# Long tails and two-block starts at the seams of a chain of layers: four units of weights held at a part's end, three units of two blocks at its beginning

## The chip, the cores and the metric

The kernel runs on 1 core of one Trainium2 chip. The metric is the time of one execution on the device, in microseconds (us). Engines are named as in the profile: PE is TensorE (PEld its weight loads), DVE VectorE, ACT ScalarE, POOL GpSimd, SP the queue that issues most DMAs.

## The reference

One sequence of 256 tokens with 1024 features, all in float32, goes through two networks of two layers each, one behind the other.

```python
def first_block(x, ...):                       # two layers
    for l in range(2):
        x = x + 0.5 * swiglu_ffn(rmsnorm(x, ffn1_norm[l]), ffn1_w_up[l], ffn1_w_down[l])
        x = x + mixer(rmsnorm(x, mix_norm[l]), w_in[l], b_in[l], ...)
        x = x + 0.5 * swiglu_ffn(rmsnorm(x, ffn2_norm[l]), ffn2_w_up[l], ffn2_w_down[l])
        x = rmsnorm(x, final_norm[l])

def second_block(x, c, ...):                   # two layers, h is scaled and shifted by mod
    mod = silu(c) @ mod_w[i] + mod_b[i]
    h = rms_norm(x, norm_mix_pre[i]) * (1.0 + sc_m) + sh_m
    y = mixer_ab(h, ...) if i == 0 else mixer_c(h, ...)
    x = x + (1.0 + g_m) * rms_norm(y, norm_mix_post[i])
    h = rms_norm(x, norm_ffn_pre[i]) * (1.0 + sc_f) + sh_f
    x = x + (1.0 + g_f) * rms_norm(conv_ffn(h, ...), norm_ffn_post[i])
```

`swiglu_ffn` is `(silu(h @ up_a) * (h @ up_b)) @ down` with 2816 hidden features. `mixer` adds three groups of banded attention and a convolution module: a gated input, a convolution over 31 tokens on 1024 channels, a layer norm over the channels, SiLU and a projection. `mixer_ab` joins a gated linear recurrence (a causal convolution over 4 tokens, two gates by 64x64 blocks, a scan) with a compressed, selected and windowed attention; `mixer_c` is a gated causal convolution over 3 tokens; `conv_ffn` a gated network whose gate passes a causal convolution over 3 tokens.

## The kernel before

Ten **parts** stand in a row: ffn1, mixer, ffn2 for each of two layers, then mixer_ab, conv_ffn, mixer_c, conv_ffn. Each begins with a norm of x, which is held in the tile `xres` as two **halves** of 128 tokens (h0, h1), and ends with a projection whose result is added to x.

Every product with a float32 weight is three matmuls: weights and activations are split into a rounded part (`hi`, `xh`, on ACT or DVE) and a rest (`lo`, `xl`, on DVE or POOL), and hi*xh, lo*xh and hi*xl are summed. A **unit** is four row blocks of 128 by 512 columns of a weight (1 MB): one DMA into `raw` (3 buffers), a cast to `hi`, a subtraction to `lo` (3 buffers of each). The first three units of each part are "fine" (`self.fine`): their `lo` is made by POOL in four quarters of 128x512. One unit is 24 matmuls of 128x512 in the form `xs`, 12 for each half of the tokens, into one sum for each half (tokens by columns). A block of 512 output columns is two units for a weight with 1024 rows, six for ffn's w_down and conv_ffn's down. The form `ws` has the weights stationary and gives columns by tokens, in matmuls of 128x256; where columns by tokens are wanted of an `xs` block, `first_block` copies its result on ACT (L928) and turns it on PE (eight transposes, L931).

A part's seam works thus. `xs_units` runs the last TAIL = 2 units of a projection's second half of columns first for h0 and then for h1, so that h0's norm can start while PE works on h1 (18 matmuls in ffn and conv_ffn, where the last unit has two row blocks, 24 elsewhere). The norm goes over ACT and DVE (sums of squares, `hr`, `rstd`, `xn`), PE transposes `xn` (L264, result `tp`), ACT and DVE make `xh` and `xl` (L269, L270, L276, L278, L279), and the next part's first block starts with two units for h0 and then h1 (`xs_units` with tail 2, or `first_block`). In ffn with `nxt` and `out` (ffn2 of layer 1, before mixer_ab) `scale_x` (L323) scales each half of x for the residual directly behind its `next_xT`.

The order of each engine's instructions is fixed when the kernel is built, by a scheduler that goes by priorities and by the order of the code. Side work is handed out by `pump`, a few tasks behind each unit of weights: the steps of mixer's convolution (L623, DVE, one tap on a channel block each), the `mod` products (L853, DVE, on 1 MB loads of mod_w, in ffn1 and ffn2) and the recurrence's gates in mixer_ab (L1122 on PE, then ACT and DVE). In mixer, ORDER lists the blocks: G a gate of the convolution's input, A its value (with A0 the convolution can begin), two digits or x8 a block of queries, keys or values, a and g, c the attention and the later gates. Behind the convolution stands its layer norm: sums on POOL (L611, `u`), a mean by PE (L716), a subtraction (L719), squares, sums on POOL (`lns`), a sum by PE (L731), and at its end `cTh` (L499), which the convolution's projection needs.

Of the kernel before, what the change touches and what calls it, by code (L numbers as in the profile page):

```python
# [11 lines left out]
F32R = mybir.dt.float32r  # L12
# [16 lines left out]
ORDER = "G0 A0 04 00 G1 A1 02 x8 06 a0 10 g0 16 12 14 a1 g2 g1 c g3".split()  # L29
# [6 lines left out]
TAIL = 2  # L36
# [8 lines left out]
class Net:  # L45
# [78 lines left out]
    def weights(self, src, heads=False):  # L124
# [7 lines left out]
        if not heads:  # L132
            return self.split_raw(raw, kk, n)
# [229 lines left out]
    def xs_units(self, units, tail=0):  # L363
        acc = [self.mmt(), self.mmt()]
        n = len(units)
        tail = min(tail, n)
        for i, (xt, k0, src) in enumerate(units[: n - tail]):
            self.xs(acc, xt, k0, self.weights(src), i == 0, i == n - 1)
        last = [(i, u, self.weights(u[2])) for i, u in enumerate(units) if i >= n - tail]
# [3 lines left out]
        return acc  # L373

# [4 lines left out]
    def ffn(self, norm, w_up, w_down, extra=None, then=None, pre=None, final=None, nxt=None):  # L379
        self.fine = FINE  # L380
        self.cut = 1 if then else None
        out = []
# [3 lines left out]
        with ExitStack() as es:  # L386
            hp = es.enter_context(tc.tile_pool(name="ffnh", bufs=1))
            wp = es.enter_context(tc.tile_pool(name="ffnw", bufs=4))
# [3 lines left out]
            if extra:  # L392
                mp = es.enter_context(tc.tile_pool(name="modp", bufs=1))
# [3 lines left out]
            for c0 in range(0, DFF, 512):  # L397
                n = min(512, DFF - c0)
                ac = {}
                if n < 512:  # L400
# [5 lines left out]
                    ac = {0: acc, DFF: [a[:, n:] for a in acc]}  # L406
                for off in (0, DFF) if n == 512 else ():
                    ac[off] = self.xs_units(self.units(w_up, xt, off + c0, n), TAIL if off + c0 == 0 else 0)
                    if off + c0 == 0:
                        self.cut = None  # L410
                        if then:
                            then()
                        if final is not None:
                            rows = hp.tile([P, D], F32, name="fb")
                            nc.sync.dma_start(rows, final.partition_broadcast(P))
                        self.bg["mod"].extend(tasks)
# [86 lines left out]
    def mixer(self, l, d, xt):  # L503
# [9 lines left out]
        with ExitStack() as es:  # L513
# [24 lines left out]
            def qkv(e, i0, head=False):  # L538
# [5 lines left out]
                acc = [self.mmt(), self.mmt()]  # L544
                ws = []
                for k0 in (0, 4):
                    src = w9[:, k0 : k0 + 4, i0] if both else w9[:, k0 : k0 + 4, i0 : i0 + 2, e]
# [996 lines left out]
```

## Time and profile before

| | us |
|---|---|
| median of 3 runs (2185.32 to 2195.68) | 2190.9 |
| profiled execution | 2186.2 |
| its span | 2184.4 |
| PE busy | 2123.1 (97%) |
| DVE busy | 1433.4 (66%) |
| ACT busy | 1142.0 (52%) |
| POOL busy | 537.4 (25%) |

The table is read from the page of the profiled execution and the times of the runs. PE is busy nearly all the time, so a gain is to be looked for in the stretches in which it isn't, and in those in which its clock is low.

### The profile page before, as it was taken

Reading aid. Unit: us, or ns where it says so; the run is one execution under the profiler, and the core shown is the slowest. Engines: PE = TensorE matmul, PEld = TensorE weight load, DVE = VectorE, ACT = ScalarE, POOL = GpSimd, SP = SyncE. Lnnn points to the kernel's source line nnn. Section 1 sums busy time; section 2 is a strip of 40 time slices with the busy share of each in tenths; the row PEclk is TensorE's granted clock in tenths of the full one; section 3 lists DMA queues with packets and bytes.
Section 4 is the critical chain, followed back from the end, with each engine's and each line's share of the span. In section 5 each row is a group of like instructions: output and inputs, shape, how many; then the busy total and the mean of one; then the engine's idle time right before and its main releaser. Section 6 shows DMA issues by size and latency. Waiting matters only on the chain.

```text
span 2184.4 us, 30473 instructions
## 1 busy us (share of the span) xinstructions
PE 2123.1 (97%) x11966; PEld 1810.9 (83%) x11966; DVE 1433.4 (66%) x2343; ACT 1142.0 (52%) x1578; POOL 537.4 (25%) x431
## 2 busy tenths in 40 slices
PE   8999999999999999999999999999999999999998
PEld 6887988888887788798888888778877998797997
DVE  6844788857877654488876785575555665566663
ACT  5435545565443443554565544576666544546452
POOL 3003985532001200488652200230002000202000
PEclk9999999999999999999999999999999999999999
DMA  9865553437988555466334886565223646554553
GB/s 350 315 205 170 183 191 124 140 135 263 346 302 292 178 177 182 154 197 209 112 111 155 302 315 186 165 158 178 85 78 106 197 144 210 169 188 158 180 177 112
DMA packets 233152, 415.04 MB, mean 190 GB/s; under 512 B 16048, under 2 KB 74288, under 8 KB 233008
## 3 DMA queue, kind: packets, MB, share of 16 engines
q1 hardware_dynamic: 232208, 410.99, 56.2%
q10 hardware_dynamic: 800, 2.10, 0.3%
q8 instruction: 94, 1.54, 0.3%
q14 instruction: 50, 0.41, 0.1%
HBM read 410.94 MB, written 2.11 MB: 189 GB/s over the span
## 4 chain that ended last, share of the span: by engine, by line
PE 88%; DVE 6%; ACT 3%; DMA 2%; issue 1%; POOL 1%; SPq 0%; DVEq 0%; ACTq 0%; POOLq 0%
PE mm L191 18%; PE mm L193 18%; PE mm L192 18%; PE mm L475 8%; PE mm L477 8%; PE mm L476 8%; PE sp L677 2%; PE sp L1330 1%; PE po L692 1%; DMA raw<-in_ffn_w_up 1%; PE tp L428 1%; PE tp L687 1%; DMA mraw<-in_mod_w 1%; PE tp L264 1%; DVE lo L175 1%
## 5 line engine op out<-in xcount | busy, mean ns | idle before, releaser
L171 ACT CAST hi<-raw 128x2048 fp32r<-128x2048 f32 (+2 forms) x427 | 635.8, 1502 | 516.3 <-PE mm L193 295.5
L175 POOL TENSOR_TENSOR lo<-raw,hi 128x512 fp32r<-128x512 f32 x384 | 501.4, 1338 | 1380.5 <-ACT hi L171 1087.8
L175 DVE TENSOR_TENSOR lo<-raw,hi 128x2048 fp32r<-128x2048 f32 (+1 forms) x241 | 531.2, 2205 | 338.1 <-ACT hi L171 335.5
L191 PE MATMUL mm<-hi,xh 128*128 128x512 f32 x1136 | 451.3, 398 | 8.7 <-DVE xh L278 5.3
L193 PE MATMUL mm<-hi,xl 128*128 128x512 f32 x1136 | 450.4, 397 | 1.7 <-DVE xl L270 1.7
L192 PE MATMUL mm<-lo,xh 128*128 128x512 f32 x1136 | 449.1, 395 | 0.6 <-POOL lo L175 0.3
L475 PE MATMUL mm<-xh,hi 128*128 128x256 f32 x1248 | 355.7, 285 | 0.9 <-ACT gc L763 0.4
L477 PE MATMUL mm<-xh,lo 128*128 128x256 f32 x1248 | 354.8, 284 | 0.0
L476 PE MATMUL mm<-xl,hi 128*128 128x256 f32 x1248 | 354.5, 284 | 0.0
L191 PEld LDWEIGHTS mm<-hi,xh 128*128 128x128 f32 x1136 | 216.0, 190 | 56.6 <-DVE xh L278 7.8
L193 PEld LDWEIGHTS mm<-hi,xl 128*128 128x128 f32 x1136 | 215.4, 190 | 48.3 <-DVE xl L270 3.0
L192 PEld LDWEIGHTS mm<-lo,xh 128*128 128x128 f32 x1136 | 216.0, 190 | 46.3 <-POOL lo L175 2.4
L475 PEld LDWEIGHTS mm<-xh,hi 128*128 128x128 f32 x1248 | 239.0, 192 | 2.7 <-ACT gc L763 0.8
L477 PEld LDWEIGHTS mm<-xh,lo 128*128 128x128 f32 x1248 | 239.0, 191 | 2.5 <-issue 1.3
L476 PEld LDWEIGHTS mm<-xl,hi 128*128 128x128 f32 x1248 | 239.1, 192 | 2.4 <-issue 1.3
L623 DVE SCALAR_TENSOR_TENSOR sp<-u,cols,sp 128x256 f32<-128x256 f32 x464 | 225.8, 487 | 7.8
L193 PE MATMUL mm<-hi,hl 128*128 128x512 f32 x528 | 209.9, 397 | 0.0
L191 PE MATMUL mm<-hi,hh 128*128 128x512 f32 x528 | 209.6, 397 | 0.0
L192 PE MATMUL mm<-lo,hh 128*128 128x512 f32 x528 | 209.6, 397 | 0.0
L853 DVE CUSTOM_DVE_ANT_0 mraw<-mraw,cact 128x1024 f32<-128x1024 f32 x96 | 117.6, 1254 | 12.3 <-DMA mraw<-in_mod_w 9.5
L193 PEld LDWEIGHTS mm<-hi,hl 128*128 128x128 f32 x528 | 99.6, 189 | 24.0
L192 PEld LDWEIGHTS mm<-lo,hh 128*128 128x128 f32 x528 | 99.4, 188 | 23.8
(337 smaller groups left out, 2664.8 us busy)
## 6 DMA issues: line engine op xcount, KB each, us to landing
raw<-in_ffn_w_up SPq DMA_DIRECT2D x98, 1024.0 KB, 6.1
raw<-in_ffn_w_down SPq DMA_DIRECT2D x60, 1024.0 KB, 5.0
mraw<-in_mod_w SPq DMA_DIRECT2D x48, 1024.0 KB, 7.2
raw<-in_w_in SPq DMA_DIRECT2D x72, 512.0 KB, 4.5
raw<-in_w_in SPq DMA_DIRECT2D x32, 1024.0 KB, 5.3
raw<-in_ffn_w_gate SPq DMA_DIRECT2D x20, 1024.0 KB, 5.1
raw<-in_ab_w_in SPq DMA_DIRECT2D x18, 1024.0 KB, 5.2
raw<-in_sc_w_in SPq DMA_DIRECT2D x12, 1024.0 KB, 5.1
```

Source lines behind the costliest of these rows:

```text
L171: nc.scalar.copy(hi[:, c : c + hi_step], raw[:, c : c + hi_step])
L175: eng.tensor_tensor(lo[:, bs], raw[:, bs], as32(hi[:, bs]), op=OP.subtract)
L191: nc.tensor.matmul(a, xh[:, k0 + k, t], wh[:, k], start=st, stop=False)
L192: nc.tensor.matmul(a, xh[:, k0 + k, t], wl[:, k], start=False, stop=False)
L193: nc.tensor.matmul(a, xl[:, k0 + k, t], wh[:, k], start=False, stop=en)
L264: nc.tensor.transpose(pt[:, j], src[:, k * P : k * P + P], self.ident)
L475: nc.tensor.matmul(a, wh[:, k, js], xh[:, k0 + k], start=st, stop=False, skip_group_check=True)
L476: nc.tensor.matmul(a, wh[:, k, js], xl[:, k0 + k], start=False, stop=False, skip_group_check=True)
L477: nc.tensor.matmul(a, wl[:, k, js], xh[:, k0 + k], start=False, stop=en, skip_group_check=True)
L623: dv.scalar_tensor_tensor(cv[:, ch] if j == CW - 1 else acc[:, e], src, w, acc[:, e], op0=OP.mult, op1=OP.add)
L677: nc.tensor.matmul(sc[:, o : o + n], QK[e, pr, g, hs], QK[e, pr, 3 + g, ks], start=True, stop=True)
L853: dv.tensor_tensor_reduce(r, r, self.cact, 1.0, 0.0, op0=OP.mult, op1=OP.add, accum_out=self.mod[i][:, 4 * b + 2 * u + j][:, None])
```

## The change

- `xs_units` takes `spare`: two more pairs of buffers for `hi` and `lo`. With them the tail has TAIL + 2 = 4 units. ffn's w_down, conv_ffn's down and mixer_ab's w_out pass it for their second half of columns; mixer's w_out and mixer_c's w_out don't. In ffn the room comes from pools that are closed before w_down (`ffnw` and `modp`, the buffers of `hv` and `mraw`), in mixer_ab from tiles that are done.
- `two_blocks` begins a part: two units of a first block and one of a second for h0, the same three for h1, then the fourth unit for both halves. It begins all four ffn (first blocks of both halves of w_up), mixer (G0 and 04), mixer_ab (both blocks of the recurrence's input), mixer_c and both conv_ffn. `turned_block` turns a finished block. In conv_ffn `up` and in mixer_c `cg` were `ws` blocks and are now `xs` blocks that are turned.
- In mixer G0 and 04 thus come ahead of A0.
- In ffn2 of layer 1 `scale_x` comes behind both halves' `next_xT`.
- In ffn the `mod` tasks are handed over ahead of the load of `final`'s rows.

```diff
-ORDER = "G0 A0 04 00 G1 A1 02 x8 06 a0 10 g0 16 12 14 a1 g2 g1 c g3".split()
+ORDER = "A0 00 G1 A1 02 x8 06 a0 10 g0 16 12 14 a1 g2 g1 c g3".split()
...
-    def xs_units(self, units, tail=0):
+    def xs_units(self, units, tail=0, spare=None):
         acc = [self.mmt(), self.mmt()]
         n = len(units)
-        tail = min(tail, n)
+        spare = deque(spare() if spare else ())
+        tail = min(tail + len(spare), n)
...
+    def two_blocks(self, u0, u1):
+        get = lambda u: u[2]() if callable(u[2]) else self.weights(u[2])
+        accs = [[self.mmt(), self.mmt()] for _ in range(2)]
+        first = [(0, True, u0[0], get(u0[0])), (0, False, u0[1], get(u0[1])), (1, True, u1[0], get(u1[0]))]
+        for h in range(2):
+            for i, start, (xt, k0, _), w in first:
+                self.xs([accs[i][h]], xt, k0, w, start, not start, halves=(h,))
+        self.xs(accs[1], u1[1][0], u1[1][1], get(u1[1]), False, True)
+        return accs
...
+            up.close()
+            tl = es.enter_context(tc.tile_pool(name="ffnt", bufs=1))
             for c in range(2):
                 cs = slice(c * 512, c * 512 + 512)
-                acc = self.xs_units(self.units(w_down, (hh, hl), c * 512, 512), TAIL * c)
+                units = self.units(w_down, (hh, hl), c * 512, 512)
+                acc = self.xs_units(units, TAIL * c, (lambda: self.two_units(tl)) if c else None)
...
                             self.next_xT(nt, h, s, *nxt, xn(), tmp)
-                            if out:
-                                self.scale_x(h, r)
+            if nxt and out:
+                for h in range(2):
+                    self.scale_x(h, out[h][0])
...
+            accs = self.two_blocks(
+                self.units(w_in, xt, 3 * AW + D, 512),
+                [(xt, k0, lambda k0=k0: self.weights4(w9[:, k0 : k0 + 4, 4:6, 0])) for k0 in (0, 4)],
+            )
+            glu_gate(0, self.turned_block(self.tiles(wk, [P, 512], "w", 4), accs[0]))
+            qkv(0, 4, accs[1])
...
+            accs = self.two_blocks(*(self.units(w_in, xs, blk * 512, 512) for blk in range(2)))
             for blk in range(2):
-                a = self.first_block(lambda: work([512], "q"), w_in, xs, blk * 512)
+                a = self.turned_block(lambda: work([512], "q"), accs[blk])
```

How the built order moves, at three places. The first is **SP from ffn2 to ffn1 of the next layer** (layer 0 to 1). `raw` with `in_ffn_w_down` are ffn2's last weights, `mraw` the loads of mod_w for ffn1 of layer 1. Before:

```order
L849 DMA mraw_6107<-in_mod_w 128x2x1024
L131 DMA raw_5520<-in_ffn_w_down 128x4x512
L849 DMA mraw_6141<-in_mod_w 128x2x1024
L131 DMA raw_5550<-in_ffn_w_down 128x4x512
L131 DMA raw_5580<-in_ffn_w_down 128x4x512
L849 DMA mraw_6200<-in_mod_w 128x2x1024
L131 DMA raw_5610<-in_ffn_w_down 128x4x512
```

In the changed kernel:

```order
L131 DMA raw_5779<-in_ffn_w_down 128x4x512
L131 DMA raw_5785<-in_ffn_w_down 128x2x512
L131 DMA raw_6034<-in_ffn_w_up 128x4x512
L131 DMA raw_6046<-in_ffn_w_up 128x4x512
L131 DMA raw_6058<-in_ffn_w_up 128x4x512
L131 DMA raw_6142<-in_ffn_w_up 128x4x512
L853 DMA cact_6202<-in_c 128x1024
L865 DMA mraw_6205<-in_mod_w 128x2x1024
```

All twelve loads of mod_w stood among ffn2's w_down; now they stand behind ffn1's first weights.

The second is **DVE behind the last softmax of mixer** (`sm`, layer 0; layer 1 is the same). `sp` with `u` and `cols`, and `cv` with them, are steps of the convolution, a row with x4 is four of them; `cv` with `sp` is the layer norm's subtraction. Before:

```order
L681 ISA sm_3593,mn_3594<-sp_3589,mask_288 128x512
L681 ISA mn_3594 128x1
L623 SCALAR_TENSOR_TENSOR sp_2429<-u_1546,cols_100,sp_2429 128x256
L500 TENSOR_TENSOR oT_3992<-of_1550,oT_3992 128x512
L623 SCALAR_TENSOR_TENSOR sp_2429<-u_1546,cols_100,sp_2429 128x256
L698 RECIPROCAL rd_3608<-den_3531 128x4
L623 SCALAR_TENSOR_TENSOR cv_1549<-u_1546,cols_100,sp_2429 128x256 x2
L719 TENSOR_TENSOR cv_1549<-cv_1549,sp_3868 128x512
```

In the changed kernel:

```order
L690 ISA sm_3603,mn_3604<-sp_3599,mask_362 128x512
L690 ISA mn_3604 128x1
L636 SCALAR_TENSOR_TENSOR sp_2439<-u_1556,cols_100,sp_2439 128x256
L518 TENSOR_TENSOR oT_4002<-of_1560,oT_4002 128x512
L636 SCALAR_TENSOR_TENSOR sp_2439<-u_1556,cols_100,sp_2439 128x256
L707 RECIPROCAL rd_3618<-den_3541 128x4
L636 SCALAR_TENSOR_TENSOR sp_2439<-u_1556,cols_100,sp_2439 128x256 x5
L709 TENSOR_TENSOR ov_3620<-po_3540,rd_3618 128x256
L636 SCALAR_TENSOR_TENSOR sp_2439<-u_1556,cols_100,sp_2439 128x256 x5
L518 TENSOR_TENSOR oT_4002<-of_1560,oT_4002 128x512
L636 SCALAR_TENSOR_TENSOR sp_2439<-u_1556,cols_100,sp_2439 128x256 x2
L636 SCALAR_TENSOR_TENSOR cv_1559<-u_1556,cols_100,sp_2439 128x256 x2
```

Four steps stood behind the last softmax, now sixteen do. On PE the mean's matmul (L716, now L725) moves back by some sixty rows, while the first matmul with `cTh` keeps its place.

The third is **PE at the beginning of mixer_ab**. `ident,abw` are the transposes of a turned block, `xc,wr` the recurrence's gate of a channel block, which needs that block's finished convolution; rows with `xtW` are the next block, for keys and values. Before, 48 matmuls less seven of block 1 stand between the last transposes of block 0 and these rows:

```order
L193 MATMUL mm_11938<-hi_11953,xl_11322 128x512
L931 MATMUL mm_12005<-ident,abw_12007 128x128 x2
L931 MATMUL mm_12006<-ident,abw_12007 128x128 x2
L1122 MATMUL sp_12107<-xc,wr 64x256
L931 MATMUL mm_12005<-ident,abw_12013 128x128 x2
```

In the changed kernel:

```order
L194 MATMUL mm_11836<-hi_11947,xl_11340 128x512
L958 MATMUL mm_11975<-ident,abw_11977 128x128 x2
L958 MATMUL mm_11976<-ident,abw_11977 128x128 x2
L958 MATMUL mm_11975<-ident,abw_11983 128x128 x2
L958 MATMUL mm_11976<-ident,abw_11983 128x128 x2
L1160 MATMUL sp_12129<-xc,wr 64x256
L958 MATMUL mm_12027<-ident,abw_12029 128x128 x2
L958 MATMUL mm_12028<-ident,abw_12029 128x128 x2
```

Both blocks' matmuls now stand ahead of the turning, so the first gate follows the turning of block 0 with nothing between.

## Rows read from the trace of the kernel before

**Rows 1.** The page: busy us of each engine, share of the span, instructions.

```profile
PE 2123.1 (97%) x11966; PEld 1810.9 (83%) x11966; DVE 1433.4 (66%) x2343; ACT 1142.0 (52%) x1578; POOL 537.4 (25%) x431
```

**Rows 2.** Windows: stretch, its us, busy time by engine, PE clock, DMA share, GB/s.

```profile
201.00:221.00 20.00, 18.06 (x92) 13.73 (x91) 11.69 (x25) 13.77 (x31) 13.80 (x12) 1.00 0.48 158
459.00:475.00 16.00, 12.06 (x81) 11.63 (x80) 10.80 (x13) 12.15 (x15) 0.00 (x0) 0.79 0.58 201
702.00:745.00 43.00, 35.43 (x151) 27.75 (x150) 34.88 (x83) 21.77 (x40) 15.87 (x10) 0.92 0.62 200
...
1402.00:1428.00 26.00, 19.81 (x81) 14.85 (x80) 19.32 (x42) 16.86 (x42) 15.04 (x13) 0.87 0.40 131
1430.00:1462.00 32.00, 32.00 (x166) 22.57 (x164) 29.77 (x63) 25.49 (x48) 13.50 (x15) 1.00 0.77 176
1674.00:1696.00 22.00, 17.61 (x80) 13.15 (x79) 16.64 (x33) 15.71 (x43) 11.72 (x9) 1.00 0.44 139
1876.00:1900.00 24.00, 19.31 (x86) 14.73 (x85) 16.78 (x29) 17.44 (x39) 11.30 (x8) 0.86 0.44 149
1977.00:2002.00 25.00, 20.44 (x89) 15.74 (x88) 17.10 (x29) 17.29 (x40) 11.25 (x8) 0.86 0.39 133
```

**Rows 3.** DVE in order of time, ffn2 to ffn1: start, us, instruction, idle before it.

```profile
700.08 1.89 DVE L853 CUSTOM_DVE_ANT_0 mraw<-mraw,cact 128x1024 f32<-128x1024 f32 x1 [1.69 <-DMA mraw<-in_mod_w]
...
704.12 0.68 DVE L441 SCALAR_TENSOR_TENSOR xres<-mm,xres 128x512 f32<-128x512 f32 x1
705.59 0.69 DVE L336 TENSOR_TENSOR xres<-xres,fb 128x512 f32<-128x512 f32 x1 [0.79 <-ACT junk L207]
```

**Rows 4.** PE in order of time, ffn2 of layer 1 to mixer_ab.

```profile
1402.59 0.39 PE L191 MATMUL mm<-hi,hh 128*128 128x512 f32 x1
...
1406.56 0.40 PE L193 MATMUL mm<-hi,hl 128*128 128x512 f32 x1
1409.26 0.66 PE L264 MATMUL tp<-ident,xn 128*128 128x128 f32 x4 [2.30 <-DVE xn L350]
1410.76 0.63 PE L264 MATMUL tp<-ident,xn 128*128 128x128 f32 x4 [0.84 <-DVE xn L350]
1413.27 0.80 PE L191 MATMUL mm<-hi,xh 128*128 128x512 f32 x1 [1.89 <-DVE xh L278]
```

**Rows 5.** DVE in order of time, the same stretch.

```profile
1402.79 0.69 DVE L441 SCALAR_TENSOR_TENSOR xres<-mm,xres 128x512 f32<-128x512 f32 x1 [7.49 <-PE mm L193]
...
1407.75 2.86 DVE L350 TENSOR_SCALAR xn<-xres,rstf 128x512 f32<-128x512 f32 x2
1410.53 1.88 DVE L323 TENSOR_SCALAR xres<-xres,rstd 128x512 f32<-128x512 f32 x2
...
1421.21 0.88 DVE L350 TENSOR_SCALAR xn<-xres,rstf 128x512 f32<-128x512 f32 x2
```

**Rows 6.** POOL in order of time, the same stretch.

```profile
1406.42 5.32 POOL L175 TENSOR_TENSOR lo<-raw,hi 128x512 fp32r<-128x512 f32 x4 [2.03 <-issue]
1415.22 4.47 POOL L175 TENSOR_TENSOR lo<-raw,hi 128x512 fp32r<-128x512 f32 x3 [3.48 <-ACT hi L171]
```

**Rows 7.** PE's waits from 430 to 470: line, releaser, us, times, longest.

```profile
PE mm L475 <- ACT cTh L499: 3.9, 1, 3.9
PE sp L731 <- POOL lns L611: 0.9, 1, 0.9
```

**Rows 8.** DVE in order of time, behind the last softmax of mixer.

```profile
430.58 2.06 DVE L623 SCALAR_TENSOR_TENSOR sp<-u,cols,sp 128x256 f32<-128x256 f32 x4
433.31 0.69 DVE L681 CUSTOM_DVE_ANT_0 sm<-sp,mask 128x512 f32<-128x512 f32 x1 [0.68 <-PE sp L677]
```

**Rows 9.** ACT, DVE and PE in order of time, first convolution and gate of mixer_ab.

```profile
1432.33 1.10 ACT L939 ACTIVATE xc<-abw,cols 128x256 f32<-128x256 f32 x2
...
1435.60 5.59 DVE L941 SCALAR_TENSOR_TENSOR xc<-abw,cols,xc 128x254 f32<-128x254 f32 x10
...
1441.15 0.60 PE L931 MATMUL mm<-ident,abw 128*128 128x128 f32 x4
```

More of the change, by code (lines that the diff above doesn't have):

```diff
@@ L121, in spt, with weights @@
         return self.sp.tile([P, 512], F32, tag=tag or ("sp" if self.flip else "sq"), name=f"sp{self.n}")
-    def weights(self, src, heads=False):
+    def weights(self, src, heads=False, into=None):
         nc = self.nc
@@ L359, in tiles @@
         return tile
-    def xs_units(self, units, tail=0):
+    def xs_units(self, units, tail=0, spare=None):
         acc = [self.mmt(), self.mmt()]
         n = len(units)
-        tail = min(tail, n)
+        spare = deque(spare() if spare else ())
+        tail = min(tail + len(spare), n)
         for i, (xt, k0, src) in enumerate(units[: n - tail]):
             self.xs(acc, xt, k0, self.weights(src), i == 0, i == n - 1)
-        last = [(i, u, self.weights(u[2])) for i, u in enumerate(units) if i >= n - tail]
+        last = []
+        for i, u in enumerate(units[n - tail :]):
+            last.append((n - tail + i, u, self.weights(u[2], into=spare.popleft() if spare else None)))
         for h in range(2):
@@ L406, in ffn @@
                     ac = {0: acc, DFF: [a[:, n:] for a in acc]}
+                if c0 == 0:
+                    ac[0], ac[DFF] = self.two_blocks(*(self.units(w_up, xt, off, n) for off in (0, DFF)))
                 for off in (0, DFF) if n == 512 else ():
-                    ac[off] = self.xs_units(self.units(w_up, xt, off + c0, n), TAIL if off + c0 == 0 else 0)
+                    if c0:
+                        ac[off] = self.xs_units(self.units(w_up, xt, off + c0, n))
                     if off + c0 == 0:
@@ L412, in ffn @@
                             then()
+                        self.bg["mod"].extend(tasks)
                         if final is not None:
@@ L543, in qkv @@
                 nc.sync.dma_start(bt, bsrc.partition_broadcast(P))
[L544 to L547, printed above, removed]
-                    ws.append(self.weights4(src))
-                    if not head:
-                        self.xs(acc, xt, k0, ws[-1], k0 == 0, k0 == 4)
-                for h in range(2) if head else ():
-                    for u in range(2):
-                        self.xs([acc[h]], xt, 4 * u, ws[u], u == 0, u == 1, halves=(h,))
+                if not acc:
+                    acc = [self.mmt(), self.mmt()]
+                    for k0 in (0, 4):
+                        src = w9[:, k0 : k0 + 4, i0] if both else w9[:, k0 : k0 + 4, i0 : i0 + 2, e]
+                        self.xs(acc, xt, k0, self.weights4(src), k0 == 0, k0 == 4)
                 btf = bt.rearrange("p i n -> p (i n)")
@@ L902, in project @@
             cs = slice(c * 512, c * 512 + 512)
-            acc = self.xs_units(units(c * 512), TAIL * c)
+            acc = self.xs_units(units(c * 512), TAIL * c, spare if c else None)
             for h in range(2):
@@ L1409, in mixer_ab, with spare @@
             grow = self.as_rows(big, gain, tag="qr")
-            return self.project(big, units, grow, nxt, "qn", lambda: work([2, P], "pT"))
+            def spare():
+                t = lambda n: big.tile([P, 2048], F32R, tag=n, name=f"spare{n}")
+                return [(t("W0"), t("W1")), (t("R4"), t("R1"))]
+            return self.project(big, units, grow, nxt, "qn", lambda: work([2, P], "pT"), spare)
 def _layout(inp):
```

57 lines of the change are left out of this document (33 added, 24 removed).

## The prediction

> **What bounds the kernel now.** I read the page first: PE is busy for 2123.1 us of the span of 2184.4 [rows 1]. A change that adds hardly any work to PE can win only what PE waits, 61.3 us, and what it loses where its clock is granted at half. So next came PE's waits, and they lie at the seams between the parts; for each seam I took a window with PE's busy time and granted clock [rows 2]. The reader is to see two numbers in such a row: its width less PE's busy time is the wait, and its width times one less the clock is what the low level (1.2 in place of 2.4 GHz) costs. Where the wait comes from is then read from DVE, POOL and PE in order of time [rows 3 to 6]. Waits and clock cost by seam:
> ffn1 to mixer, once per layer: 1.9 and nothing, twice. ffn2 to ffn1 of layer 1 (702 to 745): 7.6 and 43 x 0.08 = 3.4. ffn2 to mixer_ab (1402 to 1428): 6.2 and 26 x 0.13 = 3.4. mixer_ab to conv_ffn (1674): 4.4 and nothing. conv_ffn to mixer_c (1876): 4.7 and 24 x 0.14 = 3.4. mixer_c to conv_ffn (1977): 4.6 and 25 x 0.14 = 3.5. Together 31.3 of waits and 13.7 of clock, 45 us: this is all that the seams hold.
> Away from the seams two places matter. At the end of mixer, once per layer, PE waits 3.9 for `cTh` and 0.9 on the way to it [rows 7], and the clock costs 16 x 0.21 = 3.4. And from 1430 to 1462, where mixer_ab's convolution runs on DVE, PE is busy for 32.0 of 32.0 us [rows 2]: what lies there is hidden now and needs its cover.
>
> **The seams.** Take ffn2 to mixer_ab, of which I have every step. The last matmul of h0 begins at 1402.59, and 17 matmuls later it is 1406.56 [rows 4]: 0.233 each. h0's chain starts with L441 at 1402.79 [rows 5]; its first transposes run at 1409.26, 6.5 behind that, the second four wait another 0.84, and the first matmul of the next part starts at 1413.27, 10.5 behind [rows 4]. The tail of 18 matmuls covers 4.2 of it. In the change 42 matmuls (9.8 us) stand there, but the built order puts the eight transposes behind the 21st, and a matmul behind a waiting transpose waits too: 21 x 0.233 = 4.9, so 1.6 and 0.84 are left. Then 21 more matmuls carry PE past 10.5, and h0's first matmul doesn't wait. For h1, three units for h0 (36 matmuls, 8.4 us) stand where two were; h1's transposes come behind the 25th, 5.8, so 0.7 and 0.84 are left. `scale_x`, 1.88 on DVE ahead of h1's L441 [rows 5], goes behind and is off the chain. The third unit's `lo` is now wanted 24 matmuls (5.6 us) behind the tail's end, where before it had two units for both halves, 11.2 us. POOL's quarters take 5.32 / 4 = 1.33 each and four of them fill 1406.42 to 1411.74 [rows 6]; eight quarters from about a microsecond ahead of the tail's end are done 9.7 behind it, PE is there at about 9.0: 0.7. So 1.6 + 0.84 + 0.7 + 0.84 + 0.7 = 4.7 of wait is left of 6.2. I count the clock as regained, since the longest single wait falls from 2.30 to 1.6; at mixer_ab to conv_ffn 4.4 us of such waits went with a clock of 1.00 [rows 2]. Gain 9.6 - 4.7 = 4.9, between 0 and 9.6.
> POOL against DVE is the step that I weighed most. The two L350 of h0 took 2.86 while POOL's quarters ran, those of h1 0.88 behind the end of POOL's rows [rows 5, 6]: 2.0 a seam. With three units POOL works through h1's chain as well, so I gave h1 the length of h0's. The Trainium skill says (GPSIMD Engine Reference, section 8, Key points) that POOL shares its SBUF interfaces with VectorE and contends with some kinds of its instructions; the trace agrees with its factor of three on L350. Without that rule h1's chain would be 2.0 shorter and the waits for it nearly gone, and the sum would be some 6 us lower over four seams.
> conv_ffn to mixer_c and mixer_ab to conv_ffn by the same steps, with the transposes behind the 22nd and the 26th matmul: 1.4 + 0.84 + 0.4 + 0.84 + 0.7 = 4.2 left. That is 8.1 - 4.2 = 3.9 for the one and 0.2 for the other (-2 to 8 together). mixer_c to conv_ffn: w_out has no spare units, so h0 waits as before and only h1 gains cover; I take 2.0, half of its clock and 0.3 (0 to 6). ffn1 to mixer: 0.5 of 1.9, twice, 1.0 (-1 to 3.8).
> ffn2 to ffn1 is another case. Its DVE is blocked: two L853 of `mod`, the first of 1.89 behind a wait for its load, reach from 700.08 to 704.12, where h0's L441 begins [rows 3]. The order of SP shows why, since the loads of mod_w stand among w_down's; in the change all twelve come behind ffn1's first weights, where ffn1 of layer 0 has them too. From L441 to the end of L336 are 2.2 us (704.12 to 706.28) [rows 3], and the transposes of x itself stand behind the 11th matmul, 2.6. I leave 1.5 of 11.0: gain 9.5 (5 to 11).
> Gains together 4.9 + 3.9 + 0.2 + 2.0 + 1.0 + 9.5 = 21.5.
>
> **What it adds.** Three blocks become turned ones (`up` twice, `cg`): the products are the same, eight transposes each come on top, 0.60 for four [rows 9], so 1.2 less what larger matmuls save; 2.0 for the three (0 to 3.6), all on PE. At the kernel's start the third and fourth units of w_up are wanted earlier than before: 1.5, between nothing and the third unit's four quarters on POOL, 5.3 [rows 6].
>
> **mixer's layer norm.** G0 and 04 now stand ahead of A0, so the convolution begins one block later. At the last softmax 16 of its steps are left, not 4. In order of time DVE waits for PE's scores at that softmax (0.68, and at those before it) [rows 8], so it can't have caught up. Twelve steps of 2.06 / 4 = 0.51 [rows 8] end the convolution 6.2 later. Behind it stands a chain that isn't shortened: POOL's sum, the mean, L719, squares, POOL's sums, L731, `cTh`, and at each of its links PE waits already [rows 7]. The mean's matmul moves back on PE by some sixty rows, but `cTh`'s doesn't, so nothing covers it: 6.5 per layer with a little for POOL, which has quarters of `lo` ahead of its sums. 13.0 for both (6 to 18; no gain, since PE waits at the chain's end now). If the clock falls twice there, another 3.4 per layer.
>
> **mixer_ab's gates.** Before, 41 matmuls and the turning of block 1 stand on PE ahead of the first gate. In the change the gate follows the turning of block 0 at once and waits for the whole convolution of channel block 0: L939, two in 1.10, then up to six L941 at 5.59 / 10 = 0.56 [rows 9], with the copies some 4.6, of which the rest of the transposes covers 0.6. Behind the waiting gate are queued the turning of block 1 and the next block. 4.0, and 1.5 for the later gates, which share two result buffers and wait for ACT to empty them; the clock's 3.4 by half, 1.7. 7.2 (2 to 12).
>
> **Sum.** Added 2.0 + 1.5 + 13.0 + 7.2 = 23.7, gained 21.5: 2.2 slower, as good as nothing. The profiled execution (2186.2, of which 1.8 lies around its span) is 4.7 below the median of the three runs and 0.9 above the fastest; I set the sum on the middle of the two, 2188.5, and round to 2190.
>
> **The rivals.**
> (a) Faster, 2171. The layer norm's chain has slack that the rows don't show: DVE takes the twelve steps in its waits, and the gates' wait is filled. For it: DVE waits 0.68 at a softmax, again and again; against: its order is fixed, and the steps stand behind. Then only 3 and 2 of 13.0 and 7.2 are lost: 2188.5 - 21.5 + 3.5 + 5 = 2175.5, and with the rest of the seams' 45 us partly won, 2171.
> (b) Slower, 2204. The clock decides: the seams' waits stay within the same dozen microseconds, in more and smaller pieces, and the low level is granted as before at the three seams where I counted it as regained (3.4 + 3.4 + 1.7), again at mixer_ab's gates (1.7 more) and once more in each mixer (3.4 x 2). 17 more than the forecast, 2207; with part of it, 2204. It begins to decide if waits of 1.6 and less suffice. For it: at 1402 the longest was 2.30 and the clock fell; against: at 1674 it didn't.
> (c) The long tail doesn't do what it says, because spare units come late or the transposes stand too early, so that each seam keeps its old wait: 4.9 + 3.9 are lost, 2199.
>
> **How the numbers follow.** Forecast, within 0.5% (11 us, about what a measurement of this kernel can tell from no change): 0.47. (a) 0.28. (b) 0.17. (c) 0.08, of which half still reads as no change. That makes faster 0.28, same 0.50, slower 0.22. The range reaches into (a) and (b): 2172 to 2207.
>
> **What would show it.** The loads of mod_w gone from ffn2's w_down and the wait at that seam below 2; at ffn2 to mixer_ab no wait of the first matmul for `xh`, but one of 1.6 at the transposes in the tail; a wait of about 10 in place of 4.8 before `cTh`; a new wait of PE for DVE at the first gate of some 4; clock of 1.00 in the seams' windows. Wrong would be a `cTh` wait of the old size, no wait at the gate, or a low clock at the seams although their waits are shorter.

## The result and the profile after

The changed kernel takes 2216.8 us (median; 2215.4 to 2218.4), the kernel before 2190.5 in the same comparison: a ratio of 1.013, 95% interval 1.0117 to 1.0143. It is 1.3% slower, outside the forecast range of 2172 to 2207. The profiled execution took 2217.2, its span is 2215.4, 31.0 more than before.

PE's busy time first, from the page of the changed kernel (us, share of the span, instructions):

```profile
PE 2124.9 (96%) x11846; PEld 1806.6 (82%) x11846; DVE 1432.8 (65%) x2343; ACT 1147.0 (52%) x1584; POOL 527.4 (24%) x431
```

Beside [rows 1] PE works 1.8 longer and waits 90.5 in place of 61.3: of the 31.0, 29.2 are waits of PE. What PE waited for, over the whole span (line and tile that waited, releaser, us, times, longest):

```profile
PE mm L493 <- ACT cTh L517: 13.1, 2, 6.6
PE mm L493 <- ACT u L650: 9.9, 2, 5.1
PE sp L1160 <- DVE xc L968: 9.5, 1, 9.5
PE mm L493 <- DVE gv L968: 7.4, 2, 3.7
...
PE sp L725 <- POOL u L624: 5.5, 2, 2.8
...
PE mm L958 <- ACT fb L955: 4.8, 3, 1.6
...
PE sp L740 <- POOL lns L624: 3.6, 2, 1.8
```

Four of these rows have no counterpart of their size before: `u` by ACT (mixer, behind its two blocks; 0.4 for two waits before), `xc` (the first gate of mixer_ab), `gv` and `fb` (conv_ffn and mixer_c, behind their two blocks). `cTh`, `u` by POOL and `lns` are the layer norm's chain of [rows 7], now 22.2 for both layers. The same by place, in windows like those of [rows 2] (stretch, its us, busy time by engine, PE's clock, DMA share, GB/s):

```profile
201.00:221.00 20.00, 18.02 (x81) 13.87 (x80) 7.70 (x14) 9.75 (x21) 12.07 (x10) 1.00 0.41 128
221.00:250.00 29.00, 24.14 (x151) 22.24 (x150) 8.26 (x17) 15.01 (x17) 24.15 (x20) 0.88 0.48 155
452.00:490.00 38.00, 26.88 (x182) 25.94 (x181) 18.95 (x28) 21.72 (x28) 13.49 (x12) 0.82 0.35 113
720.00:750.00 30.00, 27.31 (x120) 21.08 (x120) 28.63 (x55) 17.40 (x24) 10.66 (x8) 1.00 0.88 301
1420.00:1445.00 25.00, 22.34 (x103) 17.54 (x102) 17.97 (x42) 15.64 (x41) 11.00 (x9) 1.00 0.31 96
1455.00:1475.00 20.00, 10.46 (x49) 7.07 (x48) 19.55 (x40) 11.12 (x23) 5.69 (x6) 0.74 0.79 152
...
1708.00:1720.00 12.00, 9.55 (x43) 6.91 (x43) 9.44 (x16) 6.99 (x18) 8.59 (x6) 1.00 0.46 140
1730.00:1745.00 15.00, 9.65 (x51) 8.60 (x50) 8.86 (x14) 8.47 (x12) 0.00 (x0) 0.78 0.60 208
1910.00:1925.00 15.00, 13.48 (x61) 10.16 (x60) 9.85 (x17) 9.24 (x20) 9.35 (x7) 1.00 0.53 175
1932.00:1942.00 10.00, 8.35 (x63) 7.55 (x62) 6.80 (x11) 5.93 (x9) 0.00 (x0) 1.00 0.82 291
2003.00:2025.00 22.00, 17.56 (x83) 13.64 (x82) 15.41 (x30) 15.31 (x40) 11.38 (x8) 1.00 0.47 153
2033.00:2050.00 17.00, 11.64 (x76) 10.56 (x75) 9.13 (x14) 8.60 (x13) 0.00 (x0) 0.90 0.53 185
```

Width less PE's busy time is the wait. Mixer's two stretches come again in layer 1, conv_ffn's at 1730 again at 2033, with the same waits within 0.2 (the clock of the second ones is 0.89, 0.87 and 0.90). Of the kernel before, the first stretch of mixer and the one behind conv_ffn's seam, which [rows 2] leaves out:

```profile
221.00:250.00 29.00, 29.00 (x170) 25.76 (x169) 17.22 (x37) 17.57 (x19) 28.00 (x24) 1.00 0.59 192
...
1700.00:1715.00 15.00, 15.00 (x128) 15.00 (x127) 11.39 (x14) 9.99 (x12) 0.00 (x0) 1.00 0.65 211
```

| place | wait before | wait after | clock before | clock after |
|---|---|---|---|---|
| ffn1 to mixer, each of two | 1.9 | 2.0 | 1.00 | 1.00 |
| behind mixer's two blocks, each of two | 0 | 4.9 | 1.00 | 0.88 |
| mixer's layer norm, each of two | 4.8 | 11.1 | 0.79 (of 16 us) | 0.82 (of 38 us) |
| ffn2 to ffn1 | 7.6 | 2.7 | 0.92 | 1.00 |
| ffn2 to mixer_ab | 6.2 | 2.7 | 0.87 | 1.00 |
| first gates of mixer_ab | 0 | 9.5 | 1.00 | 0.74 |
| mixer_ab to conv_ffn | 4.4 | 2.5 | 1.00 | 1.00 |
| behind conv_ffn's two blocks, each of two | 0 | 5.4 | 1.00 | 0.78, 0.90 |
| conv_ffn to mixer_c | 4.7 | 1.5 | 0.86 | 1.00 |
| behind mixer_c's two blocks | 0 | 1.7 | 1.00 | 1.00 |
| mixer_c to conv_ffn | 4.6 | 4.4 | 0.86 | 1.00 |

The seams did what they were to do: 13.6 us of waits went, and the clock is at its upper level in each of their windows. 44 us of waits came behind them, inside the parts, while some 3.5 that had stood further on in mixer_ab went. (A low clock costs nothing where PE waits anyway, so the clock's cost in a window is at most its width times one less the clock. For a layer norm this bound was 3.4 before and is 6.8 and, in layer 1, 4.9 now.)

A second account goes by time, from the end of one seam's last transposes to the end of the next one's. By it the two mixers take 15.3 and 13.8 more than before, nearly all of the 31.0; mixer_ab and the two conv_ffn take 6.3, 2.3 and 4.6 more; the first ffn2 with the ffn1 behind it takes 7.9 less, the second ffn2 3.7 less.

The layer norm's place in the order was foreseen, the gate's wait was foreseen at less than half its size, the waits behind the two blocks were not foreseen at all. Here is the one in mixer, PE and then ACT in order of time:

```profile
230.06 1.03 PE L958 MATMUL mm<-ident,w 128*128 128x128 f32 x8
235.95 0.58 PE L493 MATMUL mm<-xh,hi 128*128 128x256 f32 x1 [4.86 <-ACT u L650]
```

```profile
231.85 1.90 ACT L172 CAST hi<-raw 128x2048 fp32r<-128x2048 f32 x1 [5.07 <-DMA raw<-in_w_in]
233.76 1.28 ACT L650 ACT_TABLE_LOAD   x1
235.06 1.57 ACT L650 ACTIVATE u<-mm,cols 128x256 f32<-128x256 f32 x4
```

The waiting matmul is the first of A0. It uses nothing that `u` makes. But `u` reads the turned block G0 from an accumulator, and `mmt` hands out four accumulators in turn: two hold the turned G0, two the block 04, so A0 has none until `u` has read G0. On ACT a cast, which itself had to wait for its weights until 231.85, and the load of a table (1.28) stand ahead of `u`. That was the first theory to be tried: a block that is held in accumulators beside another takes them from the one that follows.

### The profile page after: what moved, and what is told of

Its sections match the earlier page's. It is cut to its first block, busy times and chain, and to the rows that moved or that the text cites. A ratio compares the mean times of both kernels' runs of the same rounds, so it can differ in the third digit from the quotient of the medians.

```text
span 2215.4 us, 30238 instructions
## 1 busy us (share of the span) xinstructions
PE 2124.9 (96%) x11846; PEld 1806.6 (82%) x11846; DVE 1432.8 (65%) x2343; ACT 1147.0 (52%) x1584; POOL 527.4 (24%) x431
## 4 chain that ended last, share of the span: by engine, by line
PE 86%; DVE 4%; ACT 4%; POOL 3%; issue 2%; DMA 1%; SPq 0%; DVEq 0%; ACTq 0%; POOLq 0%
PE mm L193 18%; PE mm L194 18%; PE mm L192 18%; PE mm L493 7%; PE mm L495 7%; PE mm L494 7%; POOL lo L176 2%; PE sp L686 2%; ACT hi L172 1%; PE sp L1368 1%; PE po L701 1%; PE tp L442 1%; PE tp L696 1%; PE tp L265 1%; DMA raw<-in_ffn_w_up 1%
## 5 line engine op out<-in xcount | busy, mean ns | idle before, releaser
L172 ACT CAST hi<-raw 128x2048 fp32r<-128x2048 f32 (+3 forms) x413 | 608.5, 1489 | 487.0 <-PE mm L194 262.9
L176 DVE TENSOR_TENSOR lo<-raw,hi 128x2048 fp32r<-128x2048 f32 (+1 forms) x227 | 496.0, 2189 | 292.8 <-ACT hi L172 282.6
L493 PE MATMUL mm<-xh,hi 128*128 128x256 f32 x1152 | 332.7, 289 | 17.8 <-ACT u L650 9.9
L494 PE MATMUL mm<-xl,hi 128*128 128x256 f32 x1152 | 333.2, 289 | 0.0
L495 PE MATMUL mm<-xh,lo 128*128 128x256 f32 x1152 | 331.9, 288 | 0.0
L194 PE MATMUL mm<-hi,hl 128*128 128x512 f32 x432 | 171.2, 396 | 0.0
L193 PE MATMUL mm<-lo,hh 128*128 128x512 f32 x432 | 171.1, 396 | 0.0
L192 PE MATMUL mm<-hi,hh 128*128 128x512 f32 x432 | 171.0, 396 | 0.0
L194 PEld LDWEIGHTS mm<-hi,hl 128*128 128x128 f32 x432 | 81.1, 188 | 19.5
L193 PEld LDWEIGHTS mm<-lo,hh 128*128 128x128 f32 x432 | 81.1, 188 | 19.5
```

Of the source, the lines that this page charges most:

```text
L172: nc.scalar.copy(hi[:, c : c + hi_step], raw[:, c : c + hi_step])
L176: eng.tensor_tensor(lo[:, bs], raw[:, bs], as32(hi[:, bs]), op=OP.subtract)
L192: nc.tensor.matmul(a, xh[:, k0 + k, t], wh[:, k], start=st, stop=False)
L193: nc.tensor.matmul(a, xh[:, k0 + k, t], wl[:, k], start=False, stop=False)
L194: nc.tensor.matmul(a, xl[:, k0 + k, t], wh[:, k], start=False, stop=en)
L493: nc.tensor.matmul(a, wh[:, k, js], xh[:, k0 + k], start=st, stop=False, skip_group_check=True)
```

## The experiments

All are compared with the kernel before, in rounds on the same chip; it took 2189.9 to 2190.5 in every comparison, so times of different runs are set beside each other here. All but those that say otherwise are the changed kernel with one thing undone or altered. The cuts of code are shortened, and the line in the first that stands for several says so.

### The long tails alone

```diff
-            accs = self.two_blocks(...)            # mixer, mixer_ab, conv_ffn, mixer_c, ffn
+            # shortened: every part begins as in the kernel before
```

> The changed kernel with every start as before (two units, blocks turned one by one, mixer's old order); the long tails, the room for them and the later scaling of x stay. Theory: the tails pay and the starts cost, so this run is faster than the kernel before: the seam ffn2 to ffn1 gains some 9 (mod loads moved by the pools that are closed), ffn2 to mixer_ab and conv_ffn to mixer_c some 4 each: about 2173, ratio 0.992. Rival (the tail alone is worth nothing, since the wait only passes to the second half): 2186 to 2192.

Measured 2184.7, ratio 0.9974 (0.9964 to 0.9984): faster, but by 5 and not by 18. At the seams the tails pay nearly what was expected, though at ffn2 to mixer_ab this run still waits 3.8 with a low clock (0.88), where the changed kernel waits 2.7 with none: from seam to seam, the first ffn2 with the ffn1 behind it takes 6.9 less than before, the second ffn2 4.5 and the first conv_ffn 3.9, 15 of the 17 that the theory names. Most of it is lost again elsewhere: 5.0 in the very first ffn, where PE now waits 3.4 for `hv`, and 9.9 in mixer_ab (the two profiled executions lie 1.5 apart). At mixer_ab's end a new wait shows:

```profile
PE tp L265 <- DVE yg L351: 4.3, 1, 4.3
PE tp L1422 <- DVE ov L1404: 2.0, 1, 2.0
PE po L1388 <- ACT abw L1384: 1.7, 2, 1.2
```

These are PE's waits from 1635 to 1695 of this run. The first row is the seam's own, 4.4 in smaller pieces before; `po` and `tp` with `ov` belong to the last heads of the attention; they are taken up again below.

### The starts alone

```diff
-                acc = self.xs_units(units, TAIL * c, (lambda: self.two_units(tl)) if c else None)
+                acc = self.xs_units(units, TAIL * c, None)    # and so in conv_ffn and mixer_ab
```

> The changed kernel without the spare units: the tails have two units as before, all starts as changed. Theory: the loss is that of the starts and the tails only soften it, so this is slower than the changed kernel by what the tails save, some 10: about 2227. Rival (the tails do the harm, for example by later loads of weights): 2200 or less.

Measured 2238.1, ratio 1.0212 (1.0193 to 1.0230). The tails are worth some 21 us on top of the new starts, twice what I expected. One part of this is the seam of ffn2 to ffn1 (PE's waits from 715 to 775 of this run):

```profile
PE tp L265 <- DVE xres L337: 5.7, 2, 4.0
PE tp L442 <- DVE hl L445: 3.8, 1, 3.8
```

That is [rows 3] again (two products of mod fill DVE from 718.81 to 722.86, and h0's chain begins behind them), and in the built order of this kernel the loads of mod_w stand among w_down's as before the change. So it is the spare units, with their room taken from where `mraw` lived, that push those loads behind the seam; neither the starts nor the order in which the tasks are handed over do it.

### Mixer as before

```diff
+ORDER = "G0 A0 04 00 G1 A1 02 x8 06 a0 10 g0 16 12 14 a1 g2 g1 c g3".split()
-            accs = self.two_blocks(G0, 04)
```

> The changed kernel, mixer alone begins as before (gate block alone, then A0, then 04). Theory: mixer's start is most of the loss: A0's wait for the first gate's accumulators (5.1 twice, and 6.8 at the low clock each) and the later layer norm (6 twice, and some low clock) go: 2216.8 - 10.2 - 6.8 - 12 - 4 = about 2184. Rival (the loss lies in mixer_ab and conv_ffn): 2210.

Measured 2185.8, ratio 0.9976 (0.9964 to 0.9987): 31 us of the changed kernel's time lie in mixer's start (from seam to seam the two mixers take 16.8 and 15.6 less). The stretch behind the seam and the one of the layer norm, in this run:

```profile
221.00:250.00 29.00, 29.00 (x165) 25.55 (x164) 18.48 (x40) 15.84 (x18) 27.43 (x23) 1.00 0.61 194
430.00:470.00 40.00, 34.80 (x271) 33.16 (x271) 21.46 (x37) 31.00 (x44) 18.95 (x14) 0.97 0.30 106
```

PE is busy for 29.0 of 29.0, and waits 5.2 in the layer norm, as before.

### Other banks for the first turned block

```diff
     def turned_block(self, tile, acc, other=False):
-        out = [self.mmt(), self.mmt()]
+        out = [self.spt("sp"), self.spt("sq")] if other else [self.mmt(), self.mmt()]
```

`other` is set for G0 in mixer, for the gate in conv_ffn and for `v` in mixer_c. The order of the blocks, the data and the amount of work stay.

> The changed kernel, but the first turned block of mixer, of each conv_ffn and of mixer_c goes into the two accumulator banks that scores and gates use, in place of two of the four for products. Theory: the new waits of the block behind two_blocks (5.1 twice in mixer, 3.7 twice in conv_ffn) are for a free bank, so they go with their low clock: about 2216.8 - 17.6 - 9 = 2190. Rival (those matmuls wait for data or for ACT's turn, not for a bank): the waits stay, 2214 to 2218.

Measured 2192.9, ratio 1.0015 (1.0005 to 1.0026): 24 us less than the changed kernel. The waits for `u` and `gv` are gone altogether. The windows behind mixer's two blocks, of the layer norm and behind conv_ffn's two blocks:

```profile
221.00:250.00 29.00, 27.65 (x176) 24.97 (x175) 13.79 (x29) 18.40 (x21) 27.50 (x23) 1.00 0.58 185
445.00:482.00 37.00, 25.23 (x171) 24.18 (x170) 16.60 (x26) 22.59 (x28) 14.60 (x13) 0.88 0.33 114
1716.00:1735.00 19.00, 17.40 (x131) 16.41 (x131) 12.99 (x16) 11.25 (x15) 0.00 (x0) 1.00 0.60 208
```

4.9 fell to 1.4 (and that is a transpose that waits for DVE), 5.4 to 1.6, and the clock is at its upper level at both. What PE had waited for was a free accumulator. The layer norm's 11.8 stays (10.0 in layer 1), so it has another cause. The 1.6 in conv_ffn is the copy `fb` on ACT, behind a cast; it stays too.

Not all of the 24 us is the accumulators'. From seam to seam the two mixers take 4.7 and 5.0 less, the two conv_ffn 6.8 and 5.5, mixer_c 0.3: 22.4, with 15.2 less wait. Another 1.6 came in mixer_ab, where this run alters nothing. PE's clock was low there ahead of the gate, so that PE came later to it and waited less, behind other waits:

```profile
1408.00:1436.00 28.00, 25.35 (x104) 19.87 (x103) 17.94 (x42) 15.73 (x41) 12.62 (x12) 0.88 0.35 113
```

```profile
PE sp L1164 <- DVE xc L972: 4.5, 1, 4.5
```

### Gate and value as the two blocks

```diff
-                [(xt, k0, lambda k0=k0: self.weights4(w9[:, k0 : k0 + 4, 4:6, 0])) for k0 in (0, 4)],
+                self.units(w_in, xt, 3 * AW, 512),       # A0, turned as well; 04 comes third
```

This stands on the run with other banks.

> As the run with the other banks (2192.9), but mixer's two blocks are the convolution's gate and value (G0 and A0, both turned) in place of G0 and the block 04, which comes third. Theory: the later layer norm comes from A0's place alone. The order has 8 steps of the convolution behind the last softmax in place of 16 (4 before), so the waits up to cTh fall from 12 to about 7.5 per layer: 2192.9 - 9 - 2 of clock = 2182. Rival (the chain is late for another reason, POOL's quarters or the turned blocks): waits stay at 12, 2192.

Measured 2188.5, ratio 0.9992 (0.9982 to 1.0001), 4.4 less than with other banks alone. The layer norm, with 8 steps of the convolution behind the last softmax:

```profile
445.00:478.00 33.00, 24.24 (x165) 23.45 (x164) 13.81 (x21) 20.13 (x25) 10.97 (x9) 0.84 0.37 128
```

8.8 of waits, between the 4.8 with four steps and the 11.1 with sixteen (11.8 in the run with other banks, which has fourteen there). The order thus matters, but the number of steps doesn't explain the 8.8: the eighth step ends 2.1 later behind the softmax than the fourth did, and the mean's matmul doesn't wait at all. Nearly all of the 4.0 more lies at `lns` (4.6, 0.9 before). On POOL, where before its sums stood in a row, quarters of `lo` now stand between them (the first row is before, the others this run):

```profile
448.12 2.68 POOL L611 TENSOR_TENSOR lns<-lns,sq 128x512 f32<-128x512 f32 x2
```

```profile
449.18 2.52 POOL L176 TENSOR_TENSOR lo<-raw,hi 128x512 fp32r<-128x512 f32 x2
451.65 1.28 POOL L624 TENSOR_TENSOR lns<-lns,sq 128x512 f32<-128x512 f32 x1
452.88 1.27 POOL L176 TENSOR_TENSOR lo<-raw,hi 128x512 fp32r<-128x512 f32 x1
```

Three quarters, 3.8 us: the rival's cause holds for this part. The two mixers did gain 4.8 and 4.3 from seam to seam, 9.1 of the 11 expected. But 1.6 was lost in mixer_ab, where PE waits 9.1 at the gate again and not 4.5, and some 3 in small pieces in other parts, none of which this run alters.

### The gates behind a block

```diff
+                        with tc.issue_after(step["kv"]):   # last matmul of the block of keys and values
                             nc.tensor.matmul(ps[es_, o : o + S], w[es_, ch], xc[es_, ch], ...)
```

> The changed kernel with one difference: on TensorE the recurrence's gates of mixer_ab are queued behind the first block of keys and values (48 matmuls). Theory: the wait of 9.5 at the first gate is a wait without cover, not a loss in the convolution itself, so it goes with its low clock (10.2 at half): 2216.8 - 9.5 - 5 = 2202. Rival (the block behind waits as well, for the copies on POOL or its weights, or the later gates pass the wait on): 2210 or more.

Measured 2218.2, ratio 1.0130 (1.0115 to 1.0145): no gain, and the theory fell. PE's waits from 1440 to 1700 and the windows from 1455 of this run:

```profile
PE mm L962 <- ACT abw L959: 3.5, 1, 3.5
PE tp L1218 <- DVE abw L1202: 2.6, 1, 2.6
```

```profile
1455.00:1475.00 20.00, 16.50 (x74) 13.50 (x73) 19.45 (x39) 13.04 (x22) 7.73 (x10) 0.91 0.80 186
1475.00:1500.00 25.00, 22.38 (x104) 14.53 (x103) 13.78 (x34) 14.71 (x34) 0.00 (x0) 0.86 0.59 172
```

The gate no longer waits, and PE waits 3.5 and 2.6 elsewhere with a low clock in both windows. In the first, DVE is busy for 19.5 of 20. The prediction read [rows 2] at 1430 as "PE is busy for 32.0 of 32.0"; DVE's 29.8 stands in the same row. This stretch was nearly full on both engines, and the change moved 41 matmuls of PE's cover out of it, ahead of the turning. That DVE sets the time of the gate shows in four runs with this start (the changed kernel, mixer as before, other banks, gate and value): the first gate stands 25.8 to 26.6 behind the seam's last transposes in all of them, while PE's wait for it goes from 4.5 to 9.5.

### mixer_ab as before

```diff
-            accs = self.two_blocks(*(self.units(w_in, xs, blk * 512, 512) for blk in range(2)))
+                a = self.first_block(lambda: work([512], "q"), w_in, xs, blk * 512)
```

> The changed kernel, mixer_ab alone begins as before (its two blocks one behind the other). Theory, formed on the run with the gates behind: mixer_ab's beginning is bound by DVE, and what PE does not wait at the gate it waits elsewhere, so the old start gains little: the gate's 9.5 and its clock go, but the waits at the seam (about 4 and a low clock) and at the attention's end with a long tail (some 10) come: 2214 to 2218. Rival (the gate's wait is a loss of its own, as the prediction had it): 2216.8 - 9.5 - 5 = 2202.

Measured 2223.6, ratio 1.0152 (1.0134 to 1.0170), 7 slower than the changed kernel, not faster. No wait at the gates is left, but PE waits 3.8 in place of 2.7 at the seam, with a low clock (0.89), then for a weight's `hi` and `lo` (1.7 and 1.4), and at the attention's end for `ov` (2.1) and `po` (1.7). From seam to seam this part waits 12.7, with the new start 13.1. The gates' wait was thus no loss that could be had back by undoing the start, as long as the tail is long.

### What a faster version needs

Three runs put together what had paid. The first has the long tails, two_blocks in ffn alone and every other start as before.

> Long tails everywhere and two_blocks in the four ffn alone; mixer, mixer_ab, conv_ffn and mixer_c begin as before. Theory: at these four the start costs more than it covers, so this is faster than the run with mixer's old start (2185.8): the gate's wait (8.7 and 5 of low clock), the waits for accumulators in conv_ffn (3.9 twice, low clock 3.4 twice) go, the old seams there come back with some 15: about 2175. Rival (the run with tails alone, 2184.7, shows all that is to be had): 2184 or more.

Measured 2180.5, ratio 0.9955 (0.9941 to 0.9970): 5 more than expected; the waits at mixer_ab's end came along (`ov` 2.1, `po` 1.7).

The second has two_blocks in conv_ffn and mixer_c too, with the other banks.

> Long tails; two_blocks in ffn, conv_ffn and mixer_c, there with the first turned block in the banks of scores and gates; mixer and mixer_ab begin as before. Theory: with no accumulator to wait for, the starts in conv_ffn and mixer_c pay, so this is the fastest so far: 2185.8 less 7.7 of waits, 6.8 of low clock and some 3 from mixer_ab: about 2168. Rival (their turning costs what it covers): as tails with ffn alone, 2175.

Measured 2178.5, ratio 0.9950 (0.9933 to 0.9966). The starts in conv_ffn and mixer_c gain 2.0, which the intervals don't separate from nothing. Of the 10 that were missing I looked for the cause at mixer_ab's end (PE's waits from 1635 to 1695, and the window):

```profile
PE tp L1425 <- DVE ov L1407: 3.0, 1, 3.0
...
PE po L1391 <- ACT abw L1387: 1.7, 2, 1.2
```

```profile
1635.00:1700.00 65.00, 55.85 (x255) 43.39 (x254) 34.09 (x60) 36.23 (x74) 16.42 (x12) 0.92 0.32 103
```

The third takes the spare units away from mixer_ab's w_out.

```diff
-            return self.project(big, units, grow, nxt, "qn", lambda: work([2, P], "pT"), spare)
+            return self.project(big, units, grow, nxt, "qn", lambda: work([2, P], "pT"))
```

> As the run with old mixers and other banks (2178.5), but mixer_ab's w_out without spare units. Theory: there the long tail takes matmuls of w_out away from the end of the attention, which they had filled (waits of 1.4, 3.2, 1.0, 2.9 and low clock of 10.2): these 9 and 5 go, and 3 come back at the seam: about 2168. Rival (the attention's end waits with the old start anyway): 2178.

```profile
1635.00:1700.00 65.00, 60.76 (x285) 48.04 (x285) 37.97 (x62) 37.29 (x73) 17.94 (x12) 0.95 0.41 136
```

Measured 2172.3, ratio 0.9917 (0.9901 to 0.9932): this beats both kernels, by 18 and by 44 us. PE doesn't wait for `ov` and `po` any more: matmuls of w_out stand between the last heads where the long tail had taken them away. 4.9 us of waits went in this window and 6.2 of the time (3.2 between the profiled executions); the rest of the 10 stays open. It takes the old start as well: in the changed kernel, with the new start and the long tail, PE waits for neither.

Two more variants on top gained nothing. With the very first ffn as before:

> As the run before it (short tail in mixer_ab), and the very first ffn begins as before. Theory: the start loses 1.4 with two_blocks, since the third unit's quarters on POOL come late: 1 to 2 faster than that run. Rival: no difference.

Measured 2175.4, ratio 0.9930 (0.9914 to 0.9946): 3 slower where 1 to 2 faster were expected, a difference that the intervals don't separate from nothing. The trace has a wait of 3.5 for `hv` in that ffn, as the run with tails alone has. With that and with mixer's two blocks G0 and A0:

> As the run with the first ffn as before, but mixer begins with two blocks, G0 and A0, the first turned one in the other banks. Theory: its seam gains about 1 and the layer norm loses 3.5 per layer (eight steps behind the last softmax, not four): some 4 slower than that run. Rival (the seam and the order gain more than the layer norm loses): faster.

Measured 2190.4, ratio 1.0002 (0.9992 to 1.0012): 15 slower, where 4 were expected. From seam to seam the two mixers take 5.6 and 5.3 more than in the run before it, each with 4.7 more wait: some 3.5 at the layer norm, and 1.2 at the seam ahead of mixer, which was to gain 1 and waits 2.0 in place of 0.8. That is 10.9 of the 13.4 between the profiled executions; the rest I leave open.

## Why the prediction was wrong

**Gains at the seams: right in size, 21.5 expected, between 13.6 and 27.3 measured.** 13.6 of waits went, and the low clock of all four windows with them (13.7 at most). At ffn2 to ffn1 9.5 was expected, and 4.9 of waits and up to 3.4 of clock came. (Of the twelve loads of mod_w there, ten stand among w_down's before the change; the last two, issued at 686.61 and 698.81, stand behind ffn1's first weights, and DVE's products from 700.08 on are theirs.) Two steps inside were wrong and made up for each other. The tail's transposes were to wait 1.6 and 0.84 and hardly waited, h1's were to wait 0.7 and waited 1.8. DVE and then POOL at ffn2 to mixer_ab in the changed kernel, in order of time:

```profile
1424.32 0.88 DVE L351 TENSOR_SCALAR xn<-xres,rstf 128x512 f32<-128x512 f32 x2
...
1437.03 2.86 DVE L351 TENSOR_SCALAR xn<-xres,rstf 128x512 f32<-128x512 f32 x2
```

```profile
1430.19 2.55 POOL L176 TENSOR_TENSOR lo<-raw,hi 128x512 fp32r<-128x512 f32 x2 [14.07 <-ACT hi L172]
1432.99 8.04 POOL L176 TENSOR_TENSOR lo<-raw,hi 128x512 fp32r<-128x512 f32 x6 [0.25 <-ACT hi L172]
```

Before, POOL's quarters lay beside h0's chain and those of h1 ran free; with four units held to the end, POOL gets its first `hi` later, starts at 1430.19 and lies beside h1's. The 0.88 and 2.86 of [rows 5] changed places. The Trainium skill (GPSIMD Engine Reference, section 8, Key points: POOL shares its SBUF interfaces with VectorE) agrees with both traces. The step that failed here was to hold on to h0's price although its neighbour had moved.

**What it adds: the step that failed most.** Three blocks that become turned ones were priced at 2.0, by their transposes, with 3.6 as the upper bound, and mixer's two blocks at nothing. I counted instructions and did not count accumulators. 4.9 twice in mixer and 5.4 twice in conv_ffn came, 20.6, and 1.7 in mixer_c. The run with other banks took away 14.6 of these waits and, in the parts that it alters, 22.4 us of time. This term alone is most of the 26.8 from forecast to result: with other banks the kernel takes 2192.9, 2.9 above the forecast and within its range. The kernel's start, the other term here, was right in size: 1.5 expected, PE is busy for 0.9 less in the first 35 us (24.93, 25.84 before).

**The layer norm: right in size, in part by luck.** 6.5 per layer expected, 6.3 more wait measured (11.1 in place of 4.8), and undoing the order brought the whole wait back to 5.2. But the steps in between were off. Behind the last softmax the convolution ends 9.2 later than before (12.9 behind it, 3.7 before), not 6.2, for other work of DVE stands between the twelve steps; PE reaches `cTh` only 7.5 later, 42.1 behind the softmax in place of 34.6. With eight steps POOL's quarters, "a little" in the prediction, cost more than the steps. And the low clock that was put aside as an "if" is there: its bound rose by 3.4 in layer 0 and 1.5 in layer 1.

**mixer_ab's gates: the mechanism was right, its size half, and its meaning wrong.** 4.0 for the first gate, 9.5 measured. The bounds of 2 to 12 were for the whole term with its clock, 7.2; the gate's wait with up to 5.2 of clock (20 us at 0.74) can lie beyond them, while 3.5 of waits that had stood further on went, so that mixer_ab as a whole takes 6.3 more. DVE in order of time shows the difference:

```profile
1455.43 2.80 DVE L1079 TENSOR_SCALAR lr<-lr 128x8 f32<-128x8 f32 x1
...
1458.38 2.29 DVE L176 TENSOR_TENSOR lo<-raw,hi 128x2048 fp32r<-128x2048 f32 x1
...
1460.68 2.28 DVE L176 TENSOR_TENSOR lo<-raw,hi 128x2048 fp32r<-128x2048 f32 x1
...
1464.79 0.48 DVE L968 SCALAR_TENSOR_TENSOR xc<-abw,cols,xc 128x255 f32<-128x255 f32 x1
```

The convolution's first input was there at about 1459, but two subtractions of weights and a row of small steps (`lr`) stand ahead of it on DVE. Beside POOL's casts those small steps took some 0.55 each, one beside its fill of 2.26 took 2.80, and behind that they took 0.17. I priced the chain from its input on and did not look at what is queued ahead of it on its engine. And two runs showed that the wait passes to other places when the order around it is mended.

**The clock.** It was counted as regained at the seams, which came true, but not for the reason given, shorter waits. At mixer_c to conv_ffn the wait stayed (4.6, then 4.4) and the clock went from 0.86 to 1.00; at ffn2 to mixer_ab the runs with other banks and with the gates behind wait 2.6 and 2.2, no more than the changed kernel, with a clock of 0.88 and 0.94 there. What decides it these runs don't show. At the gates the clock was counted by half. It fell anew behind mixer's two blocks (0.88) and conv_ffn's (0.78 and 0.90): where the other banks took 15.2 us of waits away, 22.4 of time went, and the 7.2 between them is PE's busy time.

**The rivals.** (a) needed slack in the layer norm that wasn't there. (b) reached 2204, and 2207 with all of it; the time lies beyond both, and mostly by another way. Of its parts the seams' low clock did not come, that at the gates and a second one in the mixers' layer norm did. (c) did not happen. That the start's own blocks would wait for each other was none of them. (The shares of no change and slower add up to 0.51 and 0.21, not 0.50 and 0.22.)

## What to carry to other kernels

Holding a second block open costs accumulators as well as buffers. Before two blocks are started together, count how many results are alive until the one after them begins, and who has to read which to set one free. A block that is moved forward to cover a seam is taken from a place behind it; look there which engines are full in the same window, and not only whether PE waits. And a wait on a step is priced from what stands ahead of that step on its own engine, in the built order, not from the step's input on.

## What the runs showed of the hardware that I had not expected

The same two scalings `xn` (L350 before, L351 now) took 0.88 or 2.86 according to whether POOL's subtractions ran beside them, in both kernels, and the change exchanged the two halves' prices without touching either instruction. Waits of PE can cost half as much again where the clock falls behind them: in the parts that the run with other banks alters, 15.2 us of waits and 22.4 us of time went together, and the clock of the windows behind the two blocks rose from 0.88 and 0.78 to 1.00. And a wait on another engine can take up a loss ahead of it: the gate of mixer_ab came at the same time behind its seam whether PE had waited 4.5 or 9.5 us for it.
